# Moving four whole-tile operations of a decoder layer's second norm from GpSimd to VectorE

## The chip, the cores and the metric

The kernel runs on one core of one Trainium2 chip. The metric is device time in microseconds (us), the time of one execution on the chip; for a single core that is the core's own time. A profile is one execution recorded by the hardware profiler; all times inside it are counted from the start of its span.

## What is computed

One decoder layer over 256 tokens of width 1024, in float32: two attention groups, a projection, a DeepNorm residual with layer norm, a gated feed-forward part with a causal convolution over three tokens, and a second DeepNorm residual with layer norm. The part that matters here is the end:

```python
alpha = (2.0 * DEPTH) ** 0.25
x = layer_norm(alpha * x + mix, ln1_g[l], ln1_b[l])
x = layer_norm(alpha * x + conv_gated_ffn(x, w_up[l], conv_w[l], conv_b[l], w_down[l]),
               ln2_g[l], ln2_b[l])
...
def conv_gated_ffn(x, w_up, conv_w, conv_b, w_down):
    h = x @ w_up
    h = conv3(h) + conv_b
    gate, up = jnp.split(h, 2, axis=-1)
    return (jax.nn.silu(gate) * up) @ w_down
```

So the output of the first norm, with its gain and bias, is used twice: as the input of the feed-forward part and as the residual of the second norm.

## The kernel before, in words

**Precision by splitting.** Every float32 matrix product is done as three products of halves: an operand is split into a high part (a cast on ScalarE, line 83, tiles `h_...`) and a low part (raw minus high on VectorE, line 84, tiles `l_...`), and TensorE (PE) adds high times high, low times high and high times low. So each 128x1024 block of weights that comes from memory by the SyncE (SP) queue into a raw tile (`r_wu`, `r_wd`) costs one cast on ScalarE (ACT) and one two-input subtraction on VectorE (DVE) before PE can use it.

**Stages.** The input projection and the attention come first, then the output projection with the first norm, and from about 114 us on the feed-forward part, which ends the kernel together with the second norm.

**The feed-forward loop.** There are NF = 22 steps, one for each 128 columns of the hidden width of 2816. Step f runs `gate(f)`: it calls `up(f, 0)` and `up(f, 1)`, each of which loads and splits a block of `w_up`, does 24 matmuls into one PSUM tile `ph` (lines 606, 607 and 610) and applies the convolution, one ACT operation (line 613) and two DVE operations (line 615) into `hc`. Then follow silu on ACT (line 622), the product `gt` on DVE (line 626), and the split of `gt` into `ghi` (ACT, line 629) and `glo` (DVE, line 630). Two steps later (LAG = 2) `down(f)` loads and splits a block of `w_down` and adds its product into the PSUM tiles `pd` (line 640).

**What sets the order.** The program is written for a scheduler that fixes, at build time, the order of instructions on each engine and the waits between them. An engine runs its own instructions in that order and stops at the first whose inputs are not there. The place of an operation in the code is therefore not its place on the engine. Weights run ahead through rings of seven raw, seven high and seven low tiles; `hc` and `gt` have two buffers each, `ghi` and `glo` eight, and the PSUM tiles of `up` four.

**The residual of the second norm.** The first norm leaves in `r` (two tiles of 128 tokens, each 128x1024) the normalised value without gain and bias. The feed-forward path gets them on the way (the transposed copies `x1T`, split into `x1hi` and `x1lo`). The residual needs them too: `r` times gain, plus bias, for both tiles, four whole-tile operations of 128x1024. Gain and bias of both norms come as the tile `lnv`, four broadcast loads written in step 4 (line 666). In the kernel before, the four operations are written in step 6 for GpSimd (POOL):

```python
if f == 6:
    for t in range(NT):
        nc.gpsimd.tensor_tensor(r[:, t, :], r[:, t, :], lnv[:, 0, :], op=ALU.mult)
        nc.gpsimd.tensor_tensor(r[:, t, :], r[:, t, :], lnv[:, 1, :], op=ALU.add)
```

(lines 667 to 670). Their result is read first at the very end, when `pd` is added to `r` (line 490).

Of the kernel before, what the change touches and what calls it, by code (L numbers as in the profile page):

```python
# [12 lines left out]
ALU = mybir.AluOpType  # L13
# [4 lines left out]
NT = S // P  # L18
# [22 lines left out]
ATTW_BUFS = 2  # L41
FILL = (8000, 1500, 1500, 1700)
EARLY = 1
RAW_BUFS, HI_BUFS, LO_BUFS = 7, 7, 7


@with_exitstack
def layer_kernel(ctx: ExitStack, tc: tile.TileContext, a, out):
    nc = tc.nc
# [245 lines left out]
    def gen_q(pr):  # L295
        pq = acc_tile(f"pq{pr}")
        for j in range(2):
            o = pq[:, j * S:(j + 1) * S]
            hs = slice((2 * pr + j) * P, (2 * pr + j + 1) * P)
            for k in range(2):  # L300
                hi, lo = uq[k]
                mm(o, hi[:, hs], chi[:, k, :], start=(k == 0), stop=False)
                yield S
                mm(o, lo[:, hs], chi[:, k, :], start=False, stop=False)
                yield S
                mm(o, hi[:, hs], clo[:, k, :], start=False, stop=(k == 1))
                yield S
        nc.vector.tensor_tensor(qT[:, 2 * pr:2 * pr + 2, :], pq.rearrange("p (h t) -> p h t", h=2), qtab, op=ALU.mult)
# [79 lines left out]
    def gen_qk(w, pr):  # L388
        hi, lo = load_split(a["w_qk"][w * 4 + pr], CH, f"wqk{w}{pr}")
        pp = acc_tile(f"pqk{w}{pr}")  # L390
        for k in range(KT):
            ks = slice(k * P, (k + 1) * P)
            for i, (wt, xt) in enumerate(((hi, xhi), (hi, xlo), (lo, xhi))):
                mm(pp[:, :S], wt[:, ks], xt[:, k, :], start=(k == 0 and i == 0), stop=(k == KT - 1 and i == 2))
                yield S
        if w:
            nc.scalar.copy(kb[:, pr, :], pp[:, :S])
        else:
            for j in range(2):
                rows = slice(j * HD, (j + 1) * HD)  # L400
                nc.scalar.copy(qz[rows, 2 * pr + j, :], pp[rows, :S])
# [4 lines left out]
    def gen_wo(k, t, cols=None):  # L406
        if not pm:
            pm.update(row_tiles("pm", 0))
        if k not in wo:
            wo[k] = load_split(a["w_o"][k], CH, f"wo{k}")  # L410
        hi, lo = wo[k]
        tk = slice(t * P, (t + 1) * P)
        for i, (st, mv) in enumerate(((aThi, hi), (aThi, lo), (aTlo, hi))):
            for o, n in cols or COLS[0][t]:
                mm(pm[t, o][:, :n], st[:, k, tk], mv[:, o:o + n],
                   start=(k == 0 and i == 0), stop=(k == KT - 1 and i == 2))
                yield n
# [3 lines left out]
    todo += [(f"q{pr}", gen_q(pr), 0) for pr in (2, 3)]  # L421
    todo += [(f"qk{w}{pr}", gen_qk(w, pr), 0) for pr in range(NP) for w in range(2)][EARLY:]
    todo += [(f"wo{k}{t}", gen_wo(k, t), 2 * k + 2) for k in range(NP) for t in range(NT)]
# [16 lines left out]
    def needs(i):  # L440
        pr = (i % H) // 2
        if i >= H:
            return [f"qk{w}{pr}" for w in range(2) if pr * 2 + w >= EARLY]
        return [f"q{pr}"] * (pr > 0) + ["k2"] * (pr > 1)

    def run(gen):
        for _ in gen:
            pass
# [3 lines left out]
    run(gen_q(0))  # L452
    for i in range(EARLY):
        run(gen_qk(i % 2, i // 2))
# [25 lines left out]
    r = acts.tile([P, NT, D], F32, tag="r", name="r")  # L480
# [106 lines left out]
    lnv = ff1.tile([P, 4, D], F32, name="lnv")  # L587
# [31 lines left out]
    def gate(f):  # L619
        hg = up(f, 0)  # L620
        hu = up(f, 1)
        silu = nc.scalar.activation(hg, hg, AF.Silu)
        if f == NF - 1:
            preload(AF.Sqrt, 2, after=silu)
        gt = ff.tile([P, S], F32, tag="gt", name=f"gt{f}")
        nc.vector.tensor_tensor(gt, hg, hu, op=ALU.mult)  # L626
        ghi = ff.tile([P, S], F32R, tag="ghi", bufs=HELD + LAG, name=f"ghi{f}")
        glo = ff.tile([P, S], F32R, tag="glo", bufs=HELD + LAG, name=f"glo{f}")
        nc.scalar.copy(ghi, gt)  # L629
        nc.vector.tensor_sub(glo, gt, ghi.bitcast(F32))  # L630
        return ghi, glo
# [15 lines left out]
    def down(f, g):  # L647
        raw = load(a["w_down"][f], CH, f"wd{f}")
        if f < NF - HELD:
            w = late_split(raw, CH, f"wd{f}", pin=f < 2)  # L650
        else:
            w = split(raw, CH, f"wd{f}", *(ff1.tile([P, CH], F32R, name=f"{c}d{f}") for c in ("h", "l")))
        down_step(f, 0, g, w)
        if f < NF - HELD:
            down_step(f, 1, g, w)
        else:
            held[f] = (g, w)

    gates = {}
    for f in range(NF):  # L660
        gates[f] = gate(f)
        if f >= LAG:
            down(f - LAG, gates.pop(f - LAG))
        if f == 4:
            for i in range(4):
                nc.sync.dma_start(lnv[:, i, :], a["ln"][i:i + 1, :].to_broadcast([P, D]))
        if f == 6:
            for t in range(NT):
                nc.gpsimd.tensor_tensor(r[:, t, :], r[:, t, :], lnv[:, 0, :], op=ALU.mult)
                nc.gpsimd.tensor_tensor(r[:, t, :], r[:, t, :], lnv[:, 1, :], op=ALU.add)  # L670
    in_order = True
    for f in range(NF - LAG, NF - 1):
        down(f, gates.pop(f))
# [105 lines left out]
```

## Time and profile before

| what | value |
|---|---|
| time, median of three runs | 316.44 us |
| the three runs | 316.51, 316.44, 314.87 us |
| the profiled execution | 315.36 us |
| its span, first to last instruction | 313.6 us |
| around the span | 1.76 us |
| mean granted TensorE clock | 0.986 |
| PE busy | 298.9 us, 95% of the span |
| DVE busy | 227.3 us, 73% |
| ACT busy | 186.8 us, 60% |
| POOL busy | 39.6 us, 13% |

Busy time is an average over stages that are bound by different things. Read it only as a hint of where to look, then go to the stage. In the rows below, a matmul's start is exact and its end is modelled, so the spacing of starts tells more than busy time does. A timeline row that merges several instructions gives the start of the first and the time from there to the end of the last. In the waits, the arrow points from the engine that stood still to the one that let it go on.

### The profile page before, as it was taken

What the parts mean: (1) busy time and instruction counts of PE and PEld (TensorE: products, weight loads), DVE (VectorE), ACT (ScalarE), POOL (GpSimd) and SP (SyncE); (2) the same over time, 40 slices, a digit from 0 to 9 for tenths busy, and PEclk for the clock granted to TensorE, in tenths of its full rate; (3) what the DMA queues carried; (4) which work ended last, traced back from release to release, by engine and by line L of the source; (5) the groups of instructions that cost most, each with busy time, mean ns of one, the idle gap of its engine ahead of it and who ended that gap; (6) DMA issues with size and microseconds to landing.
All of it is one profiled execution on the core that took longest, in us unless ns stands there. A gap on an engine that the chain in (4) does not pass through costs nothing.

```text
span 313.6 us, 5492 instructions
## 1 busy us (share of the span) xinstructions
PE 298.9 (95%) x2058; PEld 277.8 (89%) x2058; DVE 227.3 (73%) x428; ACT 186.8 (60%) x347; POOL 39.6 (13%) x47
## 2 busy tenths in 40 slices
PE   6999999999999989799999999999999999999990
PEld 5978999999888779789999999999999999999990
DVE  3779886656654596999977666776677959873386
ACT  4789987676666179845655565565557746732410
POOL 8320100025210033900000000000000000000021
PEclk9799999999999999999999999999999999999996
DMA  6999955173233007467975545555555676000003
GB/s 201 305 371 364 304 201 201 69 262 139 72 135 103 32 0 257 175 203 257 313 275 202 186 165 189 200 200 173 175 190 197 215 264 201 1 2 0 2 0 134
DMA packets 17370, 54.36 MB, mean 173 GB/s; under 512 B 1952, under 2 KB 4400, under 8 KB 17344
## 3 DMA queue, kind: packets, MB, share of 16 engines
q1 hardware_dynamic: 16992, 52.92, 48.8%
q0 software_dynamic: 352, 1.09, 1.1%
q8 instruction: 16, 0.26, 0.4%
q14 instruction: 10, 0.08, 0.1%
HBM read 52.95 MB, written 1.05 MB: 172 GB/s over the span
## 4 chain that ended last, share of the span: by engine, by line
PE 87%; DVE 8%; ACT 2%; DMA 2%; issue 1%; SPq 0%; POOL 0%; DVEq 0%
PE pd L640 18%; PE ph L606 12%; PE ph L607 12%; PE ph L610 12%; PE pqk L275 7%; PE pm L275 7%; PE po L275 3%; PE pq L275 2%; PE sca L275 2%; PE scb L275 2%; DVE l_wu L84 2%; DMA r_wc<-in_w_c 2%; PE pc L182 1%; PE pv L246 1%; PE pv L245 1%; PE pv L244 1%
## 5 line engine op out<-in xcount | busy, mean ns | idle before, releaser
L607 PE MATMUL ph<-x1hi,l_wu 128*128 128x256 f32 x352 | 86.5, 284 | 2.1 <-DVE l_wu L84 2.1
L606 PE MATMUL ph<-x1hi,h_wu 128*128 128x256 f32 x352 | 86.4, 283 | 0.7 <-ACT x1hi L553 0.7
L607 PEld LDWEIGHTS ph<-x1hi,l_wu 128*128 128x128 f32 x352 | 66.7, 189 | 2.4 <-DVE l_wu L84 2.3
L606 PEld LDWEIGHTS ph<-x1hi,h_wu 128*128 128x128 f32 x352 | 66.6, 189 | 1.0 <-ACT x1hi L553 0.9
L84 DVE TENSOR_TENSOR l_wu<-r_wu,h_wu 128x1024 fp32r<-128x1024 f32 x44 | 56.0, 1272 | 13.6 <-ACT h_wu L83 13.5
L615 DVE SCALAR_TENSOR_TENSOR hc<-ph,cw,hc 128x255 f32<-128x255 f32 (+1 forms) x88 | 41.9, 480 | 27.8 <-ACT hc L613 26.6
L83 ACT CAST h_wu<-r_wu 128x1024 fp32r<-128x1024 f32 x44 | 45.7, 1044 | 14.3 <-PE pd L640 12.8
L610 PE MATMUL ph<-x1lo,h_wu 128*128 128x256 f32 x352 | 49.5, 283 | 0.0
L610 PEld LDWEIGHTS ph<-x1lo,h_wu 128*128 128x128 f32 x352 | 45.3, 190 | 0.0
L613 ACT ACTIVATE hc<-ph,cw 128x256 f32<-128x256 f32 x44 | 24.8, 563 | 29.5 <-PE ph L610 29.5
L705 POOL TENSOR_TENSOR r<-r,lnv 128x512 f32<-128x512 f32 x1 | 1.3, 1295 | 170.1 <-ACT r L704 170.1
L640 PE MATMUL pd<-l_wd,ghi 128*128 128x512 f32 (+1 forms) x80 | 20.2, 350 | 0.6 <-DVE l_wd L84 0.6
L640 PE MATMUL pd<-h_wd,ghi 128*128 128x512 f32 (+1 forms) x80 | 20.0, 348 | 0.0
L640 PE MATMUL pd<-h_wd,glo 128*128 128x512 f32 (+1 forms) x80 | 20.0, 348 | 0.0
L629 ACT CAST ghi<-gt 128x256 fp32r<-128x256 f32 x22 | 8.9, 404 | 18.0 <-DVE gt L626 18.0
L84 DVE TENSOR_TENSOR l_wd<-r_wd,h_wd 128x1024 fp32r<-128x1024 f32 x16 | 19.6, 1222 | 0.0
L275 PE MATMUL pqk<-xlo,h_wqk 128*128 128x256 f32 x64 | 19.1, 299 | 0.0
L275 PE MATMUL pqk<-xhi,l_wqk 128*128 128x256 f32 x64 | 19.1, 299 | 0.0
L275 PE MATMUL pqk<-xhi,h_wqk 128*128 128x256 f32 x64 | 19.0, 297 | 0.0
L83 ACT CAST h_wd<-r_wd 128x1024 fp32r<-128x1024 f32 x16 | 16.6, 1039 | 0.0
L640 PEld LDWEIGHTS pd<-l_wd,ghi 128*128 128x128 f32 x80 | 13.9, 189 | 3.1 <-DVE l_wd L84 1.0
L640 PEld LDWEIGHTS pd<-h_wd,glo 128*128 128x128 f32 x80 | 14.0, 188 | 2.1
(161 smaller groups left out, 582.7 us busy)
## 6 DMA issues: line engine op xcount, KB each, us to landing
r_wu<-in_w_up SPq DMA_DIRECT2D x44, 512.0 KB, 4.1
r_wd<-in_w_down SPq DMA_DIRECT2D x22, 512.0 KB, 3.3
r_wqk<-in_w_qk SPq DMA_DIRECT2D x8, 512.0 KB, 5.8
r_wo<-in_w_o SPq DMA_DIRECT2D x8, 512.0 KB, 3.3
lnv<-in_ln SPq DMA_DIRECT2D x4, 512.0 KB, 5.6
r_wc<-in_w_c SPq DMA_DIRECT2D x8, 208.0 KB, 4.7
xraw<-in_xT SPq DMA_DIRECT2D x8, 128.0 KB, 4.7
r_wv<-in_w_v SPq DMA_DIRECT2D x2, 512.0 KB, 5.8
```

What stands on the lines that cost most here:

```text
L83: nc.scalar.copy(hi[:, c], raw[:, c])
L84: nc.vector.tensor_sub(lo[:, c], raw[:, c], hi[:, c].bitcast(F32))
L182: nc.tensor.matmul(pc[t][:, :NC0], xhi[:, k, tk], hi[:, o:o + NC0], start=(k == 0), stop=False)
L244: nc.tensor.matmul(pv[t], xhi[:, k, tk], hi[:, o:o + HALF], start=(k == 0), stop=False)
L275: ins = nc.tensor.matmul(*args, **kw)
L606: nc.tensor.matmul(ph[:, :S], hi[:, ks], x1hi[:, k, :], start=(k == 0), stop=False)
L607: nc.tensor.matmul(ph[:, :S], lo[:, ks], x1hi[:, k, :], start=False, stop=False)
L610: nc.tensor.matmul(ph[:, :S], hi[:, ks], x1lo[:, k, :], start=False, stop=(k == KT - 1))
L613: nc.scalar.activation(hc, ph[:, :S], AF.Identity, bias=c[:, 3:4], scale=c[:, 2:3])
L615: nc.vector.scalar_tensor_tensor(hc[:, j:S], ph[:, 0:S - j], c[:, 2 - j:3 - j], hc[:, j:S], op0=ALU.mult, op1=ALU.add)
L629: nc.scalar.copy(ghi, gt)
L640: ins = nc.tensor.matmul(pd[t, o][:, :n], st[:, tk], mv[:, o:o + n], start=(f == 0 and i == 0), stop=(f == NF - 1 and i == 2))
```

## The change

The four operations leave POOL and go to DVE. In the code they stand one each in steps 8, 9, 10 and 11 (RES = 8, NT = 2) instead of all four in step 6. They read and write the same tiles as before, and nothing else is edited.

```diff
 EARLY = 1
+RES = 8
...
         if f == 4:
             for i in range(4):
                 nc.sync.dma_start(lnv[:, i, :], a["ln"][i:i + 1, :].to_broadcast([P, D]))
-        if f == 6:
-            for t in range(NT):
-                nc.gpsimd.tensor_tensor(r[:, t, :], r[:, t, :], lnv[:, 0, :], op=ALU.mult)
-                nc.gpsimd.tensor_tensor(r[:, t, :], r[:, t, :], lnv[:, 1, :], op=ALU.add)
+        if RES <= f < RES + 2 * NT:
+            t, i = divmod(f - RES, 2)
+            nc.vector.tensor_tensor(r[:, t, :], r[:, t, :], lnv[:, i, :], op=(ALU.mult, ALU.add)[i])
```

POOL's end of the program, before; `x1lo` is the split at the end of the first norm, line 705 the tail of the second:

```order
L556 TENSOR_TENSOR x1lo<-x1T_1292,x1hi 128x4x128
L556 TENSOR_TENSOR x1lo<-x1T_1298,x1hi 128x4x128
L669 TENSOR_TENSOR r<-r,lnv 128x1024 x2
L670 TENSOR_TENSOR r<-r,lnv 128x1024 x2
L705 TENSOR_TENSOR r<-r,lnv 128x512
L706 TENSOR_TENSOR r<-r,lnv 128x512
```

And in the changed kernel:

```order
L557 TENSOR_TENSOR x1lo<-x1T_1292,x1hi 128x4x128
L557 TENSOR_TENSOR x1lo<-x1T_1298,x1hi 128x4x128
L705 TENSOR_TENSOR r<-r,lnv 128x512
L706 TENSOR_TENSOR r<-r,lnv 128x512
L775 UNCONDITIONAL_BRANCH
```

The four operations are gone from POOL, which has nothing now between the first norm and the tail. (Lines 44 to 666 of the kernel before are one higher in the changed one.)

DVE before, from the gate product of step 3 to that of step 4; in `l_wu60` the digits are step 6 and half 0, in `hc41` step 4 and half 1:

```order
L626 TENSOR_TENSOR gt3_1697<-hc30_1657,hc31_1692 128x256
L84 TENSOR_TENSOR l_wu60_1927<-r_wu60_1924,h_wu60_1926 128x1024
L630 TENSOR_TENSOR glo3_1700<-gt3_1697,ghi3_1699 128x256
L615 SCALAR_TENSOR_TENSOR hc40_1755<-ph40_1730,cw_178,hc40_1755 128x255
L615 SCALAR_TENSOR_TENSOR hc40_1755<-ph40_1730,cw_178,hc40_1755 128x254
L84 TENSOR_TENSOR l_wu61_1962<-r_wu61_1959,h_wu61_1961 128x1024
L615 SCALAR_TENSOR_TENSOR hc41_1790<-ph41_1765,cw_178,hc41_1790 128x255
L615 SCALAR_TENSOR_TENSOR hc41_1790<-ph41_1765,cw_178,hc41_1790 128x254
L84 TENSOR_TENSOR l_wd4_2004<-r_wd4_2001,h_wd4_2003 128x1024
L626 TENSOR_TENSOR gt4_1795<-hc40_1755,hc41_1790 128x256
```

The same place in the changed kernel:

```order
L85 TENSOR_TENSOR l_wu60_1927<-r_wu60_1924,h_wu60_1926 128x1024
L631 TENSOR_TENSOR glo3_1700<-gt3_1697,ghi3_1699 128x256
L670 TENSOR_TENSOR r_1273<-r_1273,lnv_1367 128x1024
L616 SCALAR_TENSOR_TENSOR hc40_1755<-ph40_1730,cw_178,hc40_1755 128x255
L85 TENSOR_TENSOR l_wu61_1962<-r_wu61_1959,h_wu61_1961 128x1024
L616 SCALAR_TENSOR_TENSOR hc40_1755<-ph40_1730,cw_178,hc40_1755 128x254
L616 SCALAR_TENSOR_TENSOR hc41_1790<-ph41_1765,cw_178,hc41_1790 128x255
L670 TENSOR_TENSOR r_1273<-r_1273,lnv_1367 128x1024
L616 SCALAR_TENSOR_TENSOR hc41_1790<-ph41_1765,cw_178,hc41_1790 128x254
L85 TENSOR_TENSOR l_wd4_2004<-r_wd4_2001,h_wd4_2003 128x1024
L627 TENSOR_TENSOR gt4_1795<-hc40_1755,hc41_1790 128x256
```

Two of the four stand between the DVE work of step 4, and the other two stand in the same way among that of step 5. Written in steps 8 to 11, they have been brought forward to steps 4 and 5. The rows ahead of `glo3` are the same on DVE in both kernels; the order of matmuls on PE is the same throughout.

## Rows read from the trace of the kernel before

**Rows 1.** The page, busy time and share of the span by engine.
```profile
PE 298.9 (95%) x2058; PEld 277.8 (89%) x2058; DVE 227.3 (73%) x428; ACT 186.8 (60%) x347; POOL 39.6 (13%) x47
```

**Rows 2.** The chain of waits, 128 to 138 us: start, us, engine and tile.
```profile
125.41 2.68 DVE gt L626
128.09 3.33 DVE l_wu L84
131.42 2.54 DVE glo L630
...
134.35 1.15 DVE l_wd L84
...
135.54 2.48 PE pd L640 x12
```

**Rows 3.** The waits, 112 to 136 us: waiting engine, releaser, us in total, times, longest.
```profile
PE ph L607 <- DVE l_wu L84: 2.1, 1, 2.1
...
PE pd L640 <- DVE l_wd L84: 0.6, 1, 0.6
```

**Rows 4.** Timeline of PE: start, us, instruction and count, [idle before, releaser].
```profile
128.15 1.12 PE L610 MATMUL ph<-x1lo,h_wu 128*128 128x256 f32 x8
129.11 0.28 PE L606 MATMUL ph<-x1hi,h_wu 128*128 128x256 f32 x1
131.47 0.39 PE L607 MATMUL ph<-x1hi,l_wu 128*128 128x256 f32 x1 [2.08 <-DVE l_wu L84]
...
135.54 0.73 PE L640 MATMUL pd<-l_wd,ghi 128*128 128x512 f32 x2 [0.57 <-DVE l_wd L84]
...
139.89 0.29 PE L610 MATMUL ph<-x1lo,h_wu 128*128 128x256 f32 x1
...
148.44 0.76 PE L610 MATMUL ph<-x1lo,h_wu 128*128 128x256 f32 x5
...
163.73 0.28 PE L607 MATMUL ph<-x1hi,l_wu 128*128 128x256 f32 x1
```

**Rows 5.** Timeline of DVE, the same columns.
```profile
125.41 2.68 DVE L626 TENSOR_TENSOR gt<-hc,hc 128x256 f32<-128x256 f32 x1
128.01 3.40 DVE L84 TENSOR_TENSOR l_wu<-r_wu,h_wu 128x1024 fp32r<-128x1024 f32 x1
131.34 2.61 DVE L630 TENSOR_TENSOR glo<-gt,ghi 128x256 fp32r<-128x256 f32 x1
...
137.65 1.22 DVE L84 TENSOR_TENSOR l_wu<-r_wu,h_wu 128x1024 fp32r<-128x1024 f32 x1
138.78 0.42 DVE L630 TENSOR_TENSOR glo<-gt,ghi 128x256 fp32r<-128x256 f32 x1
...
150.81 1.22 DVE L84 TENSOR_TENSOR l_wu<-r_wu,h_wu 128x1024 fp32r<-128x1024 f32 x1
```

**Rows 6.** Timeline of POOL, 108 to 150 us, the same columns.
```profile
123.01 4.80 POOL L669 TENSOR_TENSOR r<-r,lnv 128x1024 f32<-128x1024 f32 x2 [6.43 <-DMA lnv<-in_ln]
127.76 5.91 POOL L670 TENSOR_TENSOR r<-r,lnv 128x1024 f32<-128x1024 f32 x2
```

**Rows 7.** Tile lnv, its users: ns min/median/max, first and last start.
```profile
L669 POOL TENSOR_TENSOR r<-r,lnv x2: 2410/2424/2437, 123.0 to 125.4; 128x1024 f32<-128x1024 f32 x2
L670 POOL TENSOR_TENSOR r<-r,lnv x2: 2577/2976/3376, 127.8 to 130.3; 128x1024 f32<-128x1024 f32 x2
```

**Rows 8.** Timeline of ACT, 120 to 129 us.
```profile
122.16 1.04 ACT L83 CAST h_wu<-r_wu 128x1024 fp32r<-128x1024 f32 x1
...
126.21 0.42 ACT L622 ACTIVATE hc<-hc 128x256 f32<-128x256 f32 x1
```

**Rows 9.** Windows: busy us (count) of PE, PEld, DVE, ACT, POOL; clock, DMA share, GB/s.
```profile
130.00:132.00 2.00, 0.53 (x4) 0.53 (x5) 2.00 (x2) 2.00 (x3) 2.00 (x2) 1.00 0.00 0
...
144.50:153.00 8.50, 8.50 (x65) 8.11 (x64) 8.46 (x13) 4.91 (x8) 0.00 (x0) 1.00 0.91 308
...
170.10:178.70 8.60, 8.60 (x65) 8.22 (x64) 6.15 (x9) 4.83 (x9) 0.00 (x0) 1.00 0.53 185
```

## The prediction

> **What bounds the kernel now.** Start at the page: PE is busy 95% of the span, DVE 73%, POOL 13% [rows 1]. So look for the places where PE stands still. In the waits between the first norm and the steady loop, two of PE's waits are for low parts of weights that DVE had not made: 2.1 us for `l_wu` and 0.6 us for `l_wd` [rows 3]. Later in the loop PE is full, as in 8.50 of 8.50 us from 144.5 [rows 9]. The chain of waits names what held DVE: from 125.41 to 133.96 it runs through three DVE operations, `gt`, `l_wu` and `glo`, at 2.68, 3.33 and 2.54 us, then through `l_wd`, and only at 135.54 back to PE [rows 2].
>
> These durations are the thing to see. The same operations a few microseconds later take 1.22 us (`l_wu`) and 0.42 us (`glo`; `gt` has the same shape) [rows 5]. So three operations worth 0.42 + 1.22 + 0.42 = 2.06 us took 2.68 + 3.40 + 2.61 = 8.69 us: 6.63 us too much. They lie beside the four POOL operations of the change, which fill 123.01 to 133.67 (127.76 + 5.91) [rows 6]. Put the ends side by side. The second POOL operation ends at 123.01 + 4.80 = 127.81, and `gt` at 128.09. The third starts at 127.76 and takes 2.58, so ends at 130.34 (the fourth starts at 130.3) [rows 7]; `l_wu` ends at 131.41, 1.07 later, which is about its own length. The fourth ends at 133.67, and `glo` at 133.95, 0.28 later. Each DVE operation with two inputs in SBUF waits out the POOL operation that runs when it starts, and does its work only then; the fourth POOL operation in turn is 1 us longer than the first, about one `l_wu`.
>
> **What it costs PE.** Two stalls look like 2.1 + 0.6 us, but a restart is slower than a running stream, so measure by the step. The low-part matmuls of `up` begin at 128.15 in step 2, 139.89 in step 3 and 148.44 in step 4 [rows 4]: 11.74 us, then 8.55 us, with the same 63 matmuls in each (two `up` of 24 and a `down` of 15). Step 2 loses 11.74 - 8.55 = **3.19 us**.
>
> **The change part by part.**
>
> *Removed from POOL:* two operations at 2.42 and two at 2.98 us in the mean, 10.8 us [rows 7]. Nothing waits for them before the tail, so this itself gives nothing; what it gives is the end of the blocking. Now walk the first microseconds without it. `gt` of step 0 starts at 125.41 as before and ends by 125.83. `l_wu` of step 2, half 1, whose cast began at 122.16 and took 1.04 us [rows 8], follows and ends by 125.83 + 1.22 = 127.05. PE wants it one spacing of 0.12 us after 129.11 [rows 4], at 129.23: 2.2 us to spare, where it was 2.2 us late (131.41). ACT is through with the silu at 126.63 [rows 8], casts `ghi` by about 127.05, and `glo` ends by 127.5. The `hc` between them (133.96 to 134.35) and `l_wd` (1.15) [rows 2] bring DVE to about 129.1; PE, running on, needs `l_wd` after the 24 matmuls of this `up` at 0.12 us, at 129.11 + 2.88, and two of `down`, past 132: 3 us to spare. Both gaps close. **-3.19 us** on the path.
>
> A bound from both sides: no more than 3.19, since no other time in this stretch is lost to it; no less than 2.35 if the second gap stayed. That split comes from the rows too: the wait on `l_wu` shifts PE from 129.23 to 131.47, 2.24, and with the slower first matmul 2.35; the rest, 0.84, belongs to `l_wd`. I take 3.19, because the slack behind both operands is over 2 us.
>
> *Added to DVE:* four operations of 128x1024 float32 with two SBUF inputs. The nearest row is `l_wu`, the same shape and operation kind: 1.22 us, so 4.9 us together. POOL is idle where they stand, so nothing should stretch them; at the far end they would take POOL's 2.42 to 3.38 us. They stand in steps 4 and 5, not 8 to 11, as the order rows show, and there DVE is full: 8.46 of 8.50 us in 144.5 to 153 [rows 9]. What hides them is DVE's lead over PE. `l_wu60` ends at 152.03 [rows 5], and PE first reads it at 163.73 [rows 4]: 11.7 us. In the changed kernel DVE comes there with 6.63 us less behind it and PE 3.19 us earlier, so the lead is up to 3.4 us longer, less the operations themselves. Even at POOL's speed, 10.8 us in all, they fit. By 170 us DVE has 8.60 - 6.15 = 2.45 us free in each step [rows 9], and the lead comes back. **0 us** on the path. If this cover were gone it would be the 4.9 us in full.
>
> *Moved waits:* the first of the four waits for `lnv`, which POOL already had at 123.01; on DVE it stands some 20 us behind that, so nothing queues behind a wait. Nobody waits for `r` before the tail. SP's queue has the same loads in the same order, and loads that wait for a raw tile freed by DVE go out earlier. ACT swaps a few operations from step 4 on, with the same work. 0 us.
>
> **The sum.** The profiled execution took 315.36 us. 315.36 - 3.19 + 0 = 312.17 us, its span 313.6 - 3.2 = 310.4. That execution lies 1.08 us under the median of the three runs shown, and 0.49 over the lowest; the same subtraction from the median gives 313.25. A median of new runs should lie between the two. I say **312.6 us**.
>
> **The rivals.**
>
> *Only the first gap closes.* `l_wd`, or another operand that was hidden behind it, is late in its place. Against: 3 us of slack by the walk above; for: the walk assumes that ACT is never late, and ACT was busy for 2.00 of 2.00 us in 130 to 132 [rows 9]. 315.36 - 2.35 = 313.0 us.
>
> *The change doesn't do what it says.* The four `lnv` loads land in the same stretch, and they stay. If the loads, not POOL's reading, stretched the DVE operations, nothing moves: 315.4 us, or 316.4 by the median. For: `gt` is stretched from 125.41 on, while loads were landing. Against: in 130 to 132 the DMA share is 0.00 [rows 9] and `l_wu` and `glo` are stretched nonetheless; and the ends that follow POOL's ends.
>
> *DVE becomes the bound, and it gets slower.* Place: steps 4 and 5, where DVE is full. Mechanism: the four operations delay every `l_wu` behind them, and PE meets a low part that is not there. It decides once they take more than the lead of 11.7 + 3.4 = 15.1 us; at 4.9 us they take a third of it. Price if there were no lead at all: 315.36 - 3.19 + 4.9 = 317.1 us. The Trainium skill (Perfetto Trace Analysis, section Optimizing Scalar/DVE Operations) holds that with DVE saturated, work may go over to Scalar or even GPSIMD, which speaks for leaving the four where they were; by that rule the outcome is this one, 317.1 us. The same section adds that the two share an SBUF read port, so that such a move might not help. The trace bears out the second half: the offloaded operations cost DVE 6.63 us of blocking where doing them itself would cost 4.9.
>
> **How the numbers follow.** Both gaps close: 0.80. Only the first: 0.08. Nothing moves: 0.08. Slower: 0.04. 0.5%, about what a measurement of this kernel can tell from no change, is 1.6 us. The first two cases lie beyond it, by 3.19 and 2.35 us, but the runs themselves spread over 1.64 us, so I keep 0.04 of their chance for a gain that measures smaller: faster 0.84, same 0.12, slower 0.04. Range: lowest run less the full gain, 314.87 - 3.19 = 311.7, and 0.3 for the scatter of new runs, 311.4; above, the highest run less the smaller gain, 316.51 - 2.35 = 314.2, with 0.2 for the same, 314.4. This leaves out the last two cases, 0.12, and little of the others.
>
> **What would show it.** In the changed profile: `gt`, `l_wu` and `glo` near 125 to 128 us at 0.42, 1.22 and 0.42 us; no wait of PE on L84 or its successor between 125 and 140; step 2 as long as step 3, 8.55 us; POOL empty from the first norm to the tail; four DVE operations of 1.2 us among steps 4 and 5, with PE busy throughout. I am wrong if the three operations stay long without POOL, if PE waits for `l_wu`, `l_wd` or a PSUM tile elsewhere in steps 3 to 8, or if step 2 shrinks and a later step grows by as much.

## The result, and the profile after

The changed kernel takes 311.59 us in the median of four runs (311.04 to 311.82), the kernel before 315.81 beside it (314.87 to 316.51, four runs): a ratio of 0.9857, with a 95% interval of 0.9827 to 0.9888, so about 4.5 us less (3.5 to 5.5). A second comparison on one chip (the first experiment below) gave 0.9878 (0.9852 to 0.9904), 3.9 us. The profiled execution took 311.68 us, its span is 309.9.

The page of the changed kernel, busy time by engine, as in [rows 1]:

```profile
PE 298.6 (96%) x2058; PEld 278.1 (90%) x2058; DVE 225.7 (73%) x432; ACT 186.6 (60%) x347; POOL 30.5 (10%) x43
```

DVE executes four instructions more and is busy 1.6 us less. The timeline of DVE shows why; it answers to [rows 5]:

```profile
125.02 0.42 DVE L627 TENSOR_TENSOR gt<-hc,hc 128x256 f32<-128x256 f32 x1
125.37 1.22 DVE L85 TENSOR_TENSOR l_wu<-r_wu,h_wu 128x1024 fp32r<-128x1024 f32 x1
126.57 0.43 DVE L631 TENSOR_TENSOR glo<-gt,ghi 128x256 fp32r<-128x256 f32 x1
...
127.44 1.22 DVE L85 TENSOR_TENSOR l_wd<-r_wd,h_wd 128x1024 fp32r<-128x1024 f32 x1
...
146.00 1.21 DVE L670 TENSOR_TENSOR r<-r,lnv 128x1024 f32<-128x1024 f32 x1
...
149.91 1.22 DVE L670 TENSOR_TENSOR r<-r,lnv 128x1024 f32<-128x1024 f32 x1
...
154.38 1.22 DVE L670 TENSOR_TENSOR r<-r,lnv 128x1024 f32<-128x1024 f32 x1
...
157.65 1.22 DVE L670 TENSOR_TENSOR r<-r,lnv 128x1024 f32<-128x1024 f32 x1
```

`gt`, `l_wu` and `glo` are back at 0.42, 1.22 and 0.43 us, and the four moved operations take 1.21 to 1.22 us each. In the timeline of PE, which answers to [rows 4], the low-part matmuls of steps 2 and 3 begin 8.55 us apart, where it was 11.74:

```profile
127.77 1.12 PE L611 MATMUL ph<-x1lo,h_wu 128*128 128x256 f32 x8
...
136.32 1.12 PE L611 MATMUL ph<-x1lo,h_wu 128*128 128x256 f32 x8
```

The waits of 112 to 140 us, which answer to [rows 3], have only the two that belong to the first norm left for PE:

```profile
PE ph L607 <- ACT x1hi L554: 0.7, 1, 0.7
...
PE x1t L541 <- DVE r L570: 0.4, 1, 0.4
```

And DVE is full with the moved operations while PE is full too (windows, columns as in [rows 9]):

```profile
144.50:153.00 8.50, 8.50 (x65) 8.12 (x64) 8.17 (x13) 4.79 (x7) 0.00 (x0) 1.00 0.85 267
```

**Where the time went.** Cut each span in three: up to the first `up` matmul (the start), from there to the first of the last eight low-part matmuls of step 21 (the loop), and the rest. These are the two cuts in the kernel before and then in the changed one:

```profile
114.61 0.39 PE L606 MATMUL ph<-x1hi,h_wu 128*128 128x256 f32 x1 [0.68 <-ACT x1hi L553]
...
292.38 1.12 PE L610 MATMUL ph<-x1lo,h_wu 128*128 128x256 f32 x8
```

```profile
114.23 0.39 PE L607 MATMUL ph<-x1hi,h_wu 128*128 128x256 f32 x1 [0.68 <-ACT x1hi L554]
...
288.82 1.12 PE L611 MATMUL ph<-x1lo,h_wu 128*128 128x256 f32 x8
```

With the ends of the spans at 313.55 and 309.91 us this gives:

| profiled execution | start | loop | rest | span |
|---|---|---|---|---|
| before | 114.61 | 177.77 | 21.17 | 313.55 |
| changed | 114.23 | 174.59 | 21.09 | 309.91 |
| difference | 0.38 | 3.18 | 0.08 | 3.64 |

The loop is 3.18 us shorter, against 3.19 forecast. The other 0.46 us lie outside the loop. The 0.08 us at the end go with the change: in all four kernels that have the four operations on POOL (the kernel before, its control and the two runs at steps 12 and 6) the rest takes 21.15 to 21.17 us, in all others 21.03 to 21.09. The start does not go with it, as the table of the experiments shows. TensorE's clock is not the same there in every execution, here in the windows of the kernel before and then of the changed one:

```profile
7.00:12.00 5.00, 4.48 (x15) 4.11 (x16) 4.15 (x9) 4.34 (x11) 3.55 (x3) 0.66 0.98 298
```

```profile
7.00:12.00 5.00, 5.00 (x23) 4.57 (x23) 4.69 (x10) 3.96 (x10) 3.72 (x3) 1.00 1.03 297
```

Granted clock 0.66 in the one and 1.00 in the other, with the same program. But the clock of this window does not decide how long the start is: the control below has 1.00 there and a start of 114.99 us, the run with half on POOL 0.66 and 114.57. Over the runs below the start scatters from 113.3 to 115.7 us, and all of it arises in the first 33 us: from the first matmul into `pqk` to the first `up` matmul every execution takes 82.73 to 82.76 us.

### The profile page after: what moved, and what is told of

Its sections match the earlier page's. It is cut to its first block, busy times and chain, and to the rows that moved or that the text cites. A ratio compares the mean times of both kernels' runs of the same rounds, so it can differ in the third digit from the quotient of the medians.

```text
span 309.9 us, 5488 instructions
## 1 busy us (share of the span) xinstructions
PE 298.6 (96%) x2058; PEld 278.1 (90%) x2058; DVE 225.7 (73%) x432; ACT 186.6 (60%) x347; POOL 30.5 (10%) x43
## 4 chain that ended last, share of the span: by engine, by line
PE 89%; DVE 4%; DMA 3%; ACT 1%; SPq 1%; issue 0%; DVEq 0%; ACTq 0%
PE pd L641 18%; PE ph L607 14%; PE ph L611 14%; PE ph L608 14%; PE pqk L276 7%; PE pm L276 7%; PE po L276 3%; DMA r_wv<-in_w_v 2%; PE pq L276 2%; PE sca L276 2%; PE scb L276 2%; DMA r_wc<-in_w_c 1%; PE pv L246 1%; PE pv L247 1%; PE pv L245 1%; DVE r L690 1%
## 5 line engine op out<-in xcount | busy, mean ns | idle before, releaser
L85 DVE TENSOR_TENSOR l_wu<-r_wu,h_wu 128x1024 fp32r<-128x1024 f32 x44 | 53.7, 1222 | 12.9 <-ACT h_wu L84 12.8
L85 DVE TENSOR_TENSOR l_wd<-r_wd,h_wd 128x1024 fp32r<-128x1024 f32 x16 | 19.5, 1222 | 0.0
L641 PEld LDWEIGHTS pd<-h_wd,ghi 128*128 128x128 f32 x80 | 14.0, 188 | 1.9
```

The costliest lines, as they stand in the source:

```text
L85: nc.vector.tensor_sub(lo[:, c], raw[:, c], hi[:, c].bitcast(F32))
L641: ins = nc.tensor.matmul(pd[t, o][:, :n], st[:, tk], mv[:, o:o + n], start=(f == 0 and i == 0), stop=(f == NF - 1 and i == 2))
```

## The experiments

Each was timed in five rounds beside the kernel before on its chip. Loop lengths come from the profiles, cut as above.

| run | start | loop | median | ratio to before (95%) |
|---|---|---|---|---|
| changed, again | 114.83 | 174.59 | 312.29 | 0.9878 (0.9852 to 0.9904) |
| left out | 114.08 | 174.59 | 311.51 | 0.9843 (0.9818 to 0.9869) |
| half on POOL | 114.57 | 174.94 | 312.44 | 0.9875 (0.9849 to 0.9902) |
| POOL, step 12 | 114.09 | 176.41 | 314.22 | 0.9933 (0.9912 to 0.9954) |
| POOL, step 6 | 113.87 | 174.58 | 311.55 | 0.9861 (0.9828 to 0.9895) |
| POOL memsets | 115.73 | 174.58 | 311.82 | 0.9875 (0.9841 to 0.9908) |
| 16 on DVE | 114.75 | 174.59 | 312.09 | 0.9876 (0.9841 to 0.9911) |
| control of before | 114.99 | 177.80 | 315.21 | 0.9986 (0.9958 to 1.0014) |
| 32 on DVE | 113.27 | 187.44 | 323.27 | 1.0244 (1.0210 to 1.0277) |

**The changed kernel again.** No edit.

> The changed kernel once more, for the size of the gain. If the blocking of VectorE in step 2 is all there is, the gain is the 3.19 us by which that step was longer than its neighbours: a ratio of about 0.990 (315.8 - 3.2 = 312.6), and whatever a run differs from that comes from the first 30 us, where the granted clock of TensorE is not the same in every execution. If the change gives something else as well, in every execution, the ratio stays near the 0.986 measured first, 4.4 us.

3.9 us, with an interval that holds both 0.990 and 0.986, so the time alone does not decide. The trace does better: the loop is 174.59 us again, to the hundredth.

**The four left out.** The residual has neither gain nor bias.

```diff
-        if RES <= f < RES + 2 * NT:
-            t, i = divmod(f - RES, 2)
-            nc.vector.tensor_tensor(r[:, t, :], r[:, t, :], lnv[:, i, :], op=(ALU.mult, ALU.add)[i])
```

> Leaves out the four residual operations (gain and bias of the first norm are missing from the residual); the loads of lnv stay. Theory (the four operations on VectorE are hidden by its lead): the same time as the changed kernel, within 0.5 us, and step 2 as long as step 3, 8.55 us. Rival A (the loads of lnv stretched the VectorE operations): gt, l_wu and glo are long again near 125 to 134 us and the time is that of the kernel before. Rival B (the operations cost time on VectorE): up to 4.9 us faster than the changed kernel.

The loop is 174.59 us: the four operations cost nothing where they stand. The loads of `lnv` are still there (they go out from 118.0 to 123.1 us, in the kernel before from 118.5 to 123.6), and the three operations are short in DVE's timeline, so the loads were not the cause:

```profile
124.88 0.42 DVE L627 TENSOR_TENSOR gt<-hc,hc 128x256 f32<-128x256 f32 x1
125.22 1.22 DVE L85 TENSOR_TENSOR l_wu<-r_wu,h_wu 128x1024 fp32r<-128x1024 f32 x1
126.43 0.43 DVE L631 TENSOR_TENSOR glo<-gt,ghi 128x256 fp32r<-128x256 f32 x1
```

**Half and half.**

```diff
-        if RES <= f < RES + 2 * NT:
+        if f == 6:
+            nc.gpsimd.tensor_tensor(r[:, 0, :], r[:, 0, :], lnv[:, 0, :], op=ALU.mult)
+            nc.gpsimd.tensor_tensor(r[:, 0, :], r[:, 0, :], lnv[:, 1, :], op=ALU.add)
+        if RES + NT <= f < RES + 2 * NT:
```

> Tile 0's two operations go back to GpSimd (written in step 6), tile 1's two stay on VectorE. Theory (a VectorE operation with two SBUF inputs waits out the one GpSimd operation that runs, and PE has 2.2 us of slack for l_wu and 3 for l_wd): only gt is stretched, to an end near 127.8 (about 2.3 us late), l_wu ends near 129.0, just when PE wants it, l_wd near 131, a good 1 us early; so 0 to 0.4 us slower than the changed kernel. Rival (the cost is in proportion to GpSimd's work): half of the gain is lost, 1.6 us slower than the changed kernel.

The loop is 0.35 us longer than the changed kernel's, inside the 0 to 0.4 expected and far from 1.6. The timelines of POOL, DVE and PE, one after the other:

```profile
123.33 2.42 POOL L669 TENSOR_TENSOR r<-r,lnv 128x1024 f32<-128x1024 f32 x1 [6.79 <-DMA lnv<-in_ln]
125.83 2.47 POOL L670 TENSOR_TENSOR r<-r,lnv 128x1024 f32<-128x1024 f32 x1
...
125.37 0.67 DVE L627 TENSOR_TENSOR gt<-hc,hc 128x256 f32<-128x256 f32 x1
125.96 3.43 DVE L85 TENSOR_TENSOR l_wu<-r_wu,h_wu 128x1024 fp32r<-128x1024 f32 x1
...
129.07 0.28 PE L607 MATMUL ph<-x1hi,h_wu 128*128 128x256 f32 x1
129.44 0.39 PE L608 MATMUL ph<-x1hi,l_wu 128*128 128x256 f32 x1
```

A detail of mine was wrong: not `gt` alone was stretched. `gt` came in at the end of the first POOL operation (125.75) and was over at 126.04; `l_wu` then waited out the whole second one (to 128.30), and ended at 129.39. PE wanted it at 129.19: a quarter of a microsecond late. So half of POOL's work cost a tenth of what all of it cost: PE's slack took up the rest.

**All four on POOL, but at step 12.** From the kernel before; the first operation on POOL reads a value of step 12.

```diff
-        if f == 6:
+        if f == 12:
+            nil = lnst[:, 1, 1, 28:29]
+            nc.gpsimd.tensor_scalar(nil, gates[f][0][:, 0:1].bitcast(F32), 0.0, 0.0, op0=ALU.mult, op1=ALU.add)
+            nc.gpsimd.tensor_tensor(lnv[:, 0, 0:1], lnv[:, 0, 0:1], nil, op=ALU.add)
             for t in range(NT):
```

> All four operations stay on GpSimd, but wait for a value of step 12 (two tiny GpSimd operations carry the dependence), so they run near 220 us, where VectorE is 12 us or more ahead of PE. Theory (what counts is not which engine does the work but when it blocks VectorE): VectorE operations beside them are stretched by some 5 to 7 us in all, PE waits for none, and the time is that of the changed kernel within 0.5 us. Rival (GpSimd reading SBUF costs the kernel wherever it stands): within 0.5 us of the kernel before.

Neither: the loop is 1.82 us longer than the changed kernel's. DVE is stretched as before, and PE does not wait beside it, but more than 30 us later. The timelines of DVE, ACT and PE:

```profile
227.22 2.40 DVE L84 TENSOR_TENSOR l_wd<-r_wd,h_wd 128x1024 fp32r<-128x1024 f32 x1
229.54 2.62 DVE L626 TENSOR_TENSOR gt<-hc,hc 128x256 f32<-128x256 f32 x1
232.08 3.43 DVE L84 TENSOR_TENSOR l_wu<-r_wu,h_wu 128x1024 fp32r<-128x1024 f32 x1
...
262.94 1.23 DVE L84 TENSOR_TENSOR ld<-r_wd,hd 128x1024 fp32r<-128x1024 f32 x1 [1.99 <-ACT hd L83]
...
261.85 1.05 ACT L83 CAST hd<-r_wd 128x1024 fp32r<-128x1024 f32 x1 [1.94 <-DMA r_wd<-in_w_down]
...
266.23 0.36 PE L606 MATMUL ph<-x1hi,h_wu 128*128 128x256 f32 x1 [0.72 <-ACT hd L83]
...
274.23 0.36 PE L606 MATMUL ph<-x1hi,h_wu 128*128 128x256 f32 x1 [0.65 <-DVE hc L615]
```

I had taken the lead of the steady loop for the lead everywhere. From about 242 us on, DVE and ACT also split the weights that are held for the end (`hd`, `ld`), and a debt made at 230 is not paid before it is called in. DVE is not full there: it stands still for 1.99 us before `ld`, until ACT has cast `hd`, and ACT stood still for 1.94 us until the load for that cast had landed. The loads are late because SP's queue waits for DVE to be done with the raw tiles, up to 5.8 us at a time where it is 2.9 in the run at step 6; the last three loads of `r_wd` go out from 257.13 us on, in the run at step 6 from 254.71. So the debt comes back to PE by way of the loads.

**All four on POOL at step 6.** The same edit with `f == 6`.

> As in the run with GpSimd's four operations held back to step 12, which was 1.9 us slower than the changed kernel by the medians: there VectorE fell some 6 us back at 224 to 235 us, and PE met two waits of 0.7 us at 266 and 274, in steps that also split the held weights. Here they wait for a value of step 6 instead and run near 170 to 182 us, early enough for VectorE, which is idle for 2.4 us in each step, to make the lost time good by about 205 us. Theory (blocking costs only what VectorE's lead does not cover): the feed-forward loop is as long as in the changed kernel, and the time within 0.5 us of it. Rival (GpSimd reading SBUF beside VectorE costs the kernel some 2 us wherever it stands): 2 us slower than the changed kernel again.

The loop is 174.58 us, that of the changed kernel. POOL, then DVE:

```profile
171.27 5.76 POOL L672 TENSOR_TENSOR r<-r,lnv 128x1024 f32<-128x1024 f32 x2 [0.16 <-POOL lnv L670]
177.00 5.93 POOL L673 TENSOR_TENSOR r<-r,lnv 128x1024 f32<-128x1024 f32 x2
...
178.04 2.62 DVE L626 TENSOR_TENSOR gt<-hc,hc 128x256 f32<-128x256 f32 x1
180.58 3.43 DVE L84 TENSOR_TENSOR l_wu<-r_wu,h_wu 128x1024 fp32r<-128x1024 f32 x1
...
195.14 1.23 DVE L84 TENSOR_TENSOR l_wu<-r_wu,h_wu 128x1024 fp32r<-128x1024 f32 x1 [0.48 <-ACT h_wu L83]
```

The same work on the same engine, with the same blocking, and no cost: by 195 us DVE has idle time again. What counted in the kernel before was not GpSimd's part in the work but when it was done.

**POOL busy without reading.** The changed kernel with memsets beside the old place.

```diff
+    spare = ff1.tile([P, D], F32, name="spare")
...
+        if f == 6:
+            nc.gpsimd.tensor_copy(spare[:, 0:1], lnv[:, 0, 0:1])
+            for _ in range(10):
+                nc.gpsimd.memset(spare, 0.0)
```

> The changed kernel with GpSimd kept busy in the same stretch as in the kernel before, by ten memsets of 128x1024 that wait for lnv: it writes SBUF and reads none of it. Theory (VectorE's second input waits for GpSimd's reading): gt, l_wu and glo near 125 to 128 us stay at 0.42, 1.22 and 0.42 us, and the time is that of the changed kernel within 0.5 us. Rival (any work of GpSimd on SBUF blocks them): they grow again by 5 us or more in all, PE waits for l_wu near 129 us, and 2 to 3 us are lost.

POOL, then DVE:

```profile
124.42 10.09 POOL L672 MEMSET spare<- 128x1024 f32 x10
...
126.51 0.43 DVE L628 TENSOR_TENSOR gt<-hc,hc 128x256 f32<-128x256 f32 x1
126.85 1.22 DVE L85 TENSOR_TENSOR l_wu<-r_wu,h_wu 128x1024 fp32r<-128x1024 f32 x1
128.07 0.43 DVE L632 TENSOR_TENSOR glo<-gt,ghi 128x256 fp32r<-128x256 f32 x1
```

Ten microseconds of POOL beside them, and not a hundredth lost; the loop is 174.58 us. So POOL's writing does not block, and what the four operations do beside it is reading. The Trainium skill (SBUF — State Buffer, section Who interferes with whom) states this: a DVE instruction with two SBUF inputs contends with a GpSimd instruction that reads SBUF, not with one that only writes. The traces of this case agree, at 3.40 us for `l_wu` beside POOL's reading against 1.22 beside the memsets.

**Sixteen operations on DVE.** Three products more behind each of the four, into a spare tile.

```diff
+    spare = ff1.tile([P, D], F32, name="spare")
...
+            for _ in range(3):
+                nc.vector.tensor_tensor(spare, r[:, t, :], lnv[:, i, :], op=ALU.mult)
```

> Adds twelve products of the same shape on VectorE (written to a spare tile that nobody reads) to the four, 16 operations of 1.22 us or 19.5 us in all, which stand in steps 4 to 10. Theory (hidden by VectorE's lead of 11 to 15 us and its 2.4 us of idle time a step, 7 steps): 0 to 0.5 us slower than the changed kernel. Rival (VectorE is the bound once it is full): the twelve cost their 14.6 us less the idle time of the seven steps left by the four, some 14.6 - 12 = 2.6 us or more.

The loop is 174.59 us. A window:

```profile
160.00:170.00 10.00, 10.00 (x77) 9.57 (x76) 10.00 (x14) 5.46 (x8) 0.00 (x0) 1.00 0.52 164
```

DVE is full for 10.00 of 10.00 us and the kernel is no slower: here a full engine is no bound as long as it has a lead.

**Thirty-two operations on DVE.** The same with `range(7)`.

> Adds 28 products on VectorE to the four: 32 operations of 1.14 us from start to start, 36.5 us, which stand in steps 4 to 12. VectorE is idle for 2.4 us in each of these nine steps, 22 us; the missing 14 us come out of its lead over PE (11.7 us at step 6, up to about 14 in the steady loop), which the steps that split the held weights from about 245 us on need as well: with VectorE some 6 us behind there, the run with GpSimd's work at step 12 lost 1.8 us of loop. Theory (hidden until the lead is used up): the loop of step 0 to 21 is longer than 174.59 us by 2 to 6 us, with waits of PE for VectorE or for a PSUM tile. Rival (VectorE's extra work is free at any size as long as PE bounds the loop): 174.6 us again.

The lead does run out, but the price was too low: the loop is 12.85 us longer, not 2 to 6. PE's timeline, and its windows:

```profile
207.10 0.58 PE L609 MATMUL ph<-x1hi,l_wu 128*128 128x256 f32 x1 [3.83 <-DVE l_wu L85]
207.48 0.41 PE L608 MATMUL ph<-x1hi,h_wu 128*128 128x256 f32 x1
207.69 0.41 PE L609 MATMUL ph<-x1hi,l_wu 128*128 128x256 f32 x1
...
224.06 0.55 PE L608 MATMUL ph<-x1hi,h_wu 128*128 128x256 f32 x1 [2.79 <-DVE hc L617]
225.10 0.58 PE L609 MATMUL ph<-x1hi,l_wu 128*128 128x256 f32 x1 [0.49 <-DVE l_wu L85]
```

```profile
207.00:210.00 3.00, 2.90 (x13) 2.90 (x14) 3.00 (x4) 0.00 (x0) 0.00 (x0) 0.50 0.60 184
...
224.00:228.00 4.00, 3.45 (x14) 3.19 (x15) 4.00 (x4) 0.42 (x1) 0.00 (x0) 0.50 0.46 130
```

The waits are 3.83 + 2.79 + 0.49 = 7.1 us. Most of the other 5.7 us is the clock: behind each of the two long waits PE runs at 0.50 for some six microseconds (207 to 213 and 224 to 230 us), with starts 0.21 us apart where they are 0.12 otherwise. (A small part is the slower first matmul after each wait, which the kernel before has at the full clock too: 2.24 us of shift there for 2.08 us of waiting.) One likely reason that the waits came out above my 6 us is the order: eight of the 32 stand together between 193 and 206 us with no split of weights among them. The order of matmuls on PE is not the changed kernel's either, from 202 to 235 us; what that adds was not tested apart.

**A control.** The kernel before with an unused constant; the same instructions in the same order.

> The kernel before with a constant that nothing uses and two statements on one line: the same instructions in the same order. It shows what two builds of one program differ by. If the first 30 us scatter by chance, its ratio is 1.000 within 0.002, and the start of the feed-forward matmuls lies between 114.0 and 115.5 us. If the kernel before has a slower start of its own kind, not its feed-forward part alone, the control shows it as well: granted clock 0.986 to 0.988 in the mean, where the other kernels show 0.990 to 0.996.

0.9986 (0.9958 to 1.0014): no difference that can be told, though the medians lie 0.84 us apart. Its twelve runs have clocks of 0.983 to 0.996 and the seventeen of the kernel before beside it 0.986 to 0.993, so the low mean clock is no mark of that program. The profile shows something else. POOL, DVE, PE:

```profile
123.99 10.82 POOL L670 TENSOR_TENSOR r<-r,lnv 128x1024 f32<-128x1024 f32 x4 [7.03 <-DVE hc L616]
...
125.77 0.91 DVE L627 TENSOR_TENSOR gt<-hc,hc 128x256 f32<-128x256 f32 x1
126.61 3.43 DVE L85 TENSOR_TENSOR l_wu<-r_wu,h_wu 128x1024 fp32r<-128x1024 f32 x1
129.96 2.63 DVE L631 TENSOR_TENSOR glo<-gt,ghi 128x256 fp32r<-128x256 f32 x1
...
132.90 2.99 DVE L85 TENSOR_TENSOR l_wd<-r_wd,h_wd 128x1024 fp32r<-128x1024 f32 x1
...
130.09 0.39 PE L608 MATMUL ph<-x1hi,l_wu 128*128 128x256 f32 x1 [0.34 <-DVE l_wu L85]
...
135.95 0.73 PE L641 MATMUL pd<-l_wd,ghi 128*128 128x512 f32 x2 [2.37 <-DVE l_wd L85]
```

Here POOL began a little later against DVE, four operations were stretched instead of three, and PE's stall fell almost wholly on `l_wd`: 0.34 and 2.37 us, against 2.08 and 0.57 in [rows 4]. The loop is 177.80 us all the same. The two stalls are one debt, called in at two places. How it is split hangs on when POOL begins, 1.78 us before `gt` here and 2.40 in the kernel before, and that differs between executions of the same instructions.

## Why the prediction was right or wrong

**The mechanism was right, step by step.** The three operations went back to their own length; step 2 became as long as step 3; POOL was empty between the norm and the tail; PE waited for nothing in the loop. The loop lost 3.18 us where 3.19 stood in the sum. That POOL's reading did it, and neither the loads nor POOL's being busy, is shown by the run without the operations (loads there, three operations short) and by the memsets.

**The size of the whole was too small.** The path gave 3.19 us and the sum 312.6 us; measured were 4.5 us (3.5 to 5.5) less and 311.59 us in the first comparison, 3.9 us (3.0 to 4.7) less and 312.29 us in the second. The step that failed is the one that turned the profile's sum into a time. It put everything outside step 2 at nothing, with no term for the start of the kernel, and allowed 0.3 us for the scatter of new runs; and it said that a median of new runs should lie between 312.17 and 313.25 us, because the median of three old runs lay higher than the profiled one. The median of 311.59 lies under both, and one of its four runs, at 311.04, under the range.

What the runs showed in its place: between the two profiled executions 3.68 us were gained, 3.18 in the loop, 0.38 in the start, 0.08 behind the loop and 0.04 around the span. The start alone scatters by 2.5 us over the traced executions (113.27 to 115.73), eight times the 0.3 allowed. In the traces that scatter does not follow the change: the four kernels with the operations on POOL start at 114.39 us in the mean, the seven others at 114.49. So it was luck how near the forecast came; the second median is 0.3 us from it, the first 1.0.

What made the medians differ by 0.7 to 1.3 us more than the 3.19 of the path stays open. The medians of the kernel before, less its loop, are 138.0 to 138.4 us, in four comparisons; those of the other kernels 135.8 to 137.8. Among these are the control, with the same instructions, at 137.4, and the run with the operations on POOL at step 6, at 137.0 like the changed kernel. This speaks against the change as the cause. But each loop was traced once, and a single comparison resolves no better than 0.8 us.

**The four operations on DVE cost 0**, as forecast: the loop without them is as long to the hundredth. They took 1.21 to 1.22 us, and stood in steps 4 and 5 while DVE was full.

**The rival of one remaining gap was built on an accident.** I split the 3.19 us into 2.35 for `l_wu` and 0.84 for `l_wd` and made the first the lower bound. The control has it nearly the other way round. The two are one debt, and with half of POOL's work left 0.35 us of it remained, neither 0.84 nor 2.35.

**The rival of a DVE that becomes the bound** has its mechanism, but its threshold was incomplete. 19.5 us of extra work, more than the 15.1 us of lead that I counted, cost nothing, because DVE's 2.4 us of idle time a step counts too; at 36.5 us the kernel is slower than before, with a ratio of 1.0244. And the lead does not cover the same everywhere: blocking by the value of step 6 cost nothing, by that of step 12 it cost 1.82 us. The rule cited there (the Trainium skill, Perfetto Trace Analysis, section Optimizing Scalar/DVE Operations: offload from a saturated DVE) would have given 317.1 us as the prediction worked it out, and did not hold here; that DVE is full did not matter, since DVE was still ahead of PE. Its other half, that moving work between two engines that share a read port might not help, is the one that the traces bear out.

## What to carry to other kernels

Work given to an idle engine is not free if the two share something: look for operations of the busy engine that are longer than their equals, and put their ends beside those of the other engine's. Then ask what the operation must wait for and when; an operation with no deadline belongs where the engine that pays has a lead, early enough to earn it back before the next stage that needs it. And measure a stall by the length of the step, not by the idle time that the trace names, since the restart and a second stall belong to the same debt.

## What the runs showed of the hardware

The blocking goes both ways, operation by operation. POOL's pairs take 4.80 us where DVE has nothing with two SBUF inputs beside the first of them, and 5.76 and 5.91 to 5.94 us where DVE does ([rows 6] and the runs at steps 12 and 6); the missing time is about that of the DVE operation that slipped in between. DVE's convolution operations, which read one of their inputs from PSUM, keep their length beside POOL: two of them take 1.00 us at 226.29 in the run at step 12, as they do at 217.74 with POOL idle.

TensorE's clock made the dearest of these runs dearer. After waits of 3.83 and 2.79 + 0.49 us the granted clock was 0.50, which is 1.2 GHz, for about 6 us each, and most of the 5.7 us that the loop lost on top of 7.1 us of waiting went there. After the waits of 2.08 us in the kernel before and 2.37 us in its control the granted clock was 1.00, which is 2.4 GHz (windows 131.5 to 133.5 and 136 to 138 us).
